# Moving two of eight depthwise convolution chunks from TensorE's banded products to ScalarE products summed on GpSimd

## The chip, the cores and the metric

The kernel runs on one core of a Trainium2 chip. The metric is the time of one launch on the device in microseconds (us). TensorE (PE), VectorE (DVE), ScalarE (ACT), GpSimd (POOL) and SyncE (SP) each work through a list of their own, in order, and wait for each other by semaphores.

## The reference

Two layers of a decoder trunk, 512 tokens of 1024 channels. Layer 0 mixes by a Conformer convolution module, layer 1 by sparse attention, and a gated feed-forward block follows each. The change concerns the convolution module alone:

```python
a, g = jnp.split(h @ w_in + b_in, 2, axis=-1)
u = a * jax.nn.sigmoid(g)
u = depthwise_causal_conv(u, w_dw, taps=31) + b_dw
mu, var = mean(u, -1), mean((u - mu)**2, -1)
u = silu((u - mu) * rsqrt(var + LN_EPS) * ln_g + ln_b)
return u @ w_out
```

All is in float32; a weight matrix product is made of three products of split halves.

## The kernel before

Channels lie on the partitions: 1024 channels are eight chunks of 128 partitions by 512 tokens, in tiles u0 to u7 with 32 columns of zeros ahead.

**Projection.** For each chunk the kernel makes a gate tile and a value tile, each of 24 matmuls (`proj_tile`, lines 282 to 284 or 398 to 400). The weights come by DMA, ScalarE takes their high half (wh, line 222) and VectorE the rest (wl, line 231), one tile ahead. `glu` (line 483) then makes u from the two: gr (line 485), sigmoid on ScalarE (486), ar (488), u (494).

**Convolution, two ways.** Chunks of `DVE_CONV` (0 and 1) are done on VectorE: 31 operations of multiply and add with a weight per partition (lines 501 and 505), the running sum cv in PSUM. They run at a low priority, so that the scheduler puts them into VectorE's gaps. Chunks of `PE_CONV` (2 to 7) are done on TensorE: u is written with the phase of the token first, goes to DRAM and comes back as uf with 16 channels by 8 phases on the partitions (`conv_pe_load`, line 514), and 80 small matmuls with banded weights make the sum (`conv_pe`, line 530, matmul at 544). The bands are loaded on GpSimd's queue into three buffers (line 458). VectorE adds the bias less a shift (548), where nb = bias - shift is made by GpSimd (line 532); ScalarE squares (550); and the result goes back to u through DRAM.

**Layer norm sums.** To keep the variance exact, a shift s, the mean over chunk 0, is taken off (`ln_shift`, line 567). VectorE chunks are shifted (582) and squared (584), and summed over channels by TensorE (lnst, line 593); chunks of TensorE are summed by phase (lng, line 605). `ln_tok` (line 609) copies lnst to rows (612) and transposes it (lnrt, 615); `ln_rows` (line 621) adds the two and makes mean and inverse deviation. Then `ln_out` normalizes chunk by chunk: a chunk of TensorE is read in phase order (line 730), a chunk of VectorE straight (732), then comes the scale (733), Silu twice (739) and the low half (725), and the output projection (lines 373 to 379) begins.

**The order.** The table `CONV_AT` says behind which projection pair (4 to 7, 8 is the end) what is given out: "c4" is the matmuls of chunk 4, "g0" the phase sums of the first TensorE chunk, "n0" and "m0" the shift and square, and the sums, of the first chunk of `LN_ORDER`, "s" the shift, "t" the transpose. From this a scheduler sets each engine's list.

Of the kernel before, what the change touches and what calls it, by code (L numbers as in the profile page):

```python
# [10 lines left out]
F32 = mybir.dt.float32  # L11
# [3 lines left out]
AF = mybir.ActivationFunctionType  # L15
ALU = mybir.AluOpType
# [3 lines left out]
P = 128  # L20
T = 512
# [5 lines left out]
TAPS = 31  # L27
# [8 lines left out]
V_BA, V_BG, V_BDW, V_LNG, V_LNB = 32, 40, 48, 56, 64  # L36
# [15 lines left out]

DVE_CONV = (0, 1)
PE_CONV = (2, 3, 4, 5, 6, 7)
LN_ORDER = (0, 1)
BAND_BUFS = 3
SPLIT = {7: 2}
EH = 2  # L60
CONV_AT = {4: ("s",), 5: ("c2", "c3"), 6: ("g0", "g1", "c4"), 7: ("g2", "n0", "c5"),
           8: ("w", "n1", "m0", "m1", "c6", "g3", "t", "c7", "g4", "g5")}
NLN = len(LN_ORDER)
PH_B = 48
NPH = PH_B + 8 * len(PE_CONV)
WARM0 = 10
# [44 lines left out]
def _two_pi_pieces():  # L111
    rest, out = 2.0 * math.pi, []
    for _ in range(4):
        e = math.floor(math.log2(rest))
        q = 2.0 ** (e - 4)
        piece = math.floor(rest / q) * q
        out.append(piece)
        rest -= piece
    out.append(float(np.float32(rest)))
    return out  # L120
# [3 lines left out]
def trunk(ctx: ExitStack, tc: tile.TileContext, A, out):  # L124
    nc = tc.nc
# [50 lines left out]
    for z in QV_ORDER:  # L176
        if z < 8:
            add("nw_q", z, 1024)
        else:
            w = VW[z - 8]  # L180
# [10 lines left out]
    def after(a, b):  # L191

        if b is not None:
            tc.add_manual_dep(a.ins, b.ins.name, mybir.DependencyInfo(
                mybir.DependencyClass.NoSync, mybir.DependencyReason.DATA), reason="order")
        return a
# [73 lines left out]
    def v(col, n=1):  # L270
        return vec[:, col:col + n]
# [140 lines left out]
    def rope_tables(new, follow):  # L412
        pos = new(I32)
        pf, n, sinT, cosT = (new(F32) for _ in range(4))
        big = 1.5 * 2.0 ** 23
        lim = 3.1415925

        def g(name, *a):
            return lambda: follow(getattr(nc.vector, name)(*a))

        yield lambda: nc.gpsimd.dma_start(pos, A["positions"].partition_broadcast(P))
        yield g("tensor_copy", pf, pos)
        yield g("tensor_scalar", pf, pf, v(V_INVF), None, ALU.mult)
        yield g("tensor_scalar", n, pf, 1.0 / (2.0 * math.pi), big, ALU.mult, ALU.add)
        yield g("tensor_scalar", n, n, -big, None, ALU.add)
        for c in _two_pi_pieces():
            yield g("scalar_tensor_tensor", pf, n, -c, pf, ALU.mult, ALU.add)
        yield g("tensor_scalar", pf, pf, lim, -lim, ALU.min, ALU.max)
        yield lambda: (follow(nc.scalar.activation(sinT, pf, AF.Sin)), follow(nc.scalar.activation(n, pf, AF.Abs)),
                       follow(nc.scalar.activation(cosT, n, AF.Sin, bias=halfpi, scale=-1.0)))  # L430
        yield g("tensor_scalar", sinT, sinT, v(V_SGN), None, ALU.mult)
        yield lambda: (nc.gpsimd.dma_start(angles[0], cosT), nc.gpsimd.dma_start(angles[1], sinT))


    def conv_module():
        acc = new_acc()
        with ExitStack() as cx:
            cp = cx.enter_context(tc.tile_pool(name="cp", bufs=1, side="right"))
            ct = cx.enter_context(tc.tile_pool(name="ct", bufs=2, side="right"))
# [6 lines left out]
            u = [cp.tile([P, 32 + T], F32, tag=f"u{i}", name=f"u{i}") for i in range(NK)]  # L446
            for i in range(NK):
                nc.gpsimd.memset(u[i][:, :32], 0.0)
            vch = [t[:, 32:] for t in u]
            vt = [None] * NK  # L450
# [4 lines left out]
            def load_band(j):  # L455
                t = cp.tile([P, 320, 16], F32, tag="bd", bufs=BAND_BUFS, name=f"bd{j}")
                for h in range(2):
                    tc.keep_in_program_order(nc.gpsimd.dma_start(t[:, 160 * h:160 * h + 160], A["bands"][j, :, 160 * h:160 * h + 160]))
                band[j] = t
# [3 lines left out]
            for k in range(NK):  # L463
# [5 lines left out]
                for m in range(2):  # L469
                    c = slice(k % 2 * 256 + m * P, k % 2 * 256 + (m + 1) * P)  # L470
# [7 lines left out]
            last = {}  # L478
# [4 lines left out]
            def glu(i, pA, pG):  # L483
# [4 lines left out]
                nc.vector.tensor_tensor(ar, pA, R, ALU.mult)  # L488
                if i in PE_CONV:
                    dst = u[i][:, 32:].rearrange("p (r t) -> p t r", r=8)  # L490
# [5 lines left out]
            def wtap(i, j):  # L496
                return wdw[:, i * TAPS + j:i * TAPS + j + 1]

            def conv_dve(i):
                c = pc.tile([P, T], F32, tag="pc", name=f"cv{i}")  # L500
                z = nc.vector.tensor_scalar(c, u[i][:, 2:2 + T], wtap(i, 0), v(V_BDW + i), ALU.mult, ALU.add)
                after(z, last.get("dve"))
                for j in range(1, TAPS):
                    dst = vch[i] if j == TAPS - 1 else c
                    last["dve"] = nc.vector.scalar_tensor_tensor(dst, u[i][:, 2 + j:2 + j + T], wtap(i, j), c,
                                                                 ALU.mult, ALU.add)
                vt[i] = vch[i]

            def views():
# [4 lines left out]
            def conv_pe_load(i):  # L514
                f = cp.tile([P, 8, 68], F32, tag="uf", bufs=len(PE_CONV), name=f"uf{i}")
                nc.gpsimd.memset(f[:, :, :4], 0.0)
                chan, phase = views()
                nc.sync.dma_start(chan, u[i][:, 32:].rearrange("p (r t) -> p r t", r=8))
                last["load"] = nc.sync.dma_start(f[:, :, 4:], phase)
                return f  # L520
# [7 lines left out]
            def conv_pe(j, i, f):  # L528
# [7 lines left out]
                for g0 in range(0, 8, n):  # L536
# [13 lines left out]
                    y = nc.scalar.activation(nb[:, gs], ce[:, gs], AF.Square)  # L550
                    if j == len(PE_CONV) - 2:
                        last["evac"] = {ALU: z, AF: y}
                if j + BAND_BUFS < len(PE_CONV):
                    load_band(j + BAND_BUFS)
                vt[i] = u[i][:, 32:].rearrange("p (r t) -> p r t", r=8)
                backs.append((vt[i], chan))
                if len(ups) == len(PE_CONV):
                    send_backs()
# [29 lines left out]
            def ln_sum(n, q):  # L588
                if n == 0:
                    sh["ps"] = pa.tile([P, T], F32, tag="pst", name="lnst", bufs=1)  # L590
                for e, z in enumerate((vch[LN_ORDER[n]], q)):
                    r0 = 64 * (n % 2) + 32 * e
# [65 lines left out]
            def after_glu(i):  # L658
                if i in PE_CONV:
                    ups[i] = conv_pe_load(i)  # L660
                else:
                    with tc.high_priority(offset=-100000):
                        conv_dve(i)

            def at(i):
                for z in CONV_AT.get(i, ()):
                    if z == "s":
                        ln_shift(LN_ORDER[0])
                    elif z == "t":
# [3 lines left out]
                    elif z[0] == "n":  # L673
                        sh[z] = ln_stat(LN_ORDER[int(z[1:])])
                    elif z[0] == "m":
# [41 lines left out]
            chain = {sh["end"].ins.engine: sh["end"]}  # L717
# [32 lines left out]
            state["behind"] = None  # L750
            pin.clear()
            acc = new_acc()
            follow = dict(chain)

            def table(dt):
                return cp.tile([P, 8, 68], dt, tag="uf", bufs=len(PE_CONV), name=nm("tab")).rearrange(
# [1414 lines left out]
```

## Time and profile before

| | |
|---|---|
| three timed runs | 1196.84, 1197.57, 1198.01 us |
| median | 1197.57 us |
| profiled execution, first to last instruction (span) | 1196.9 us; no other time of it is given |
| median less span | 0.7 us |
| instructions | 21262 |
| granted TensorE clock over the run | 0.999 |

The page gives busy time by engine, then groups of instructions as line, engine, operation, output<-inputs, shape, count, then busy time, the mean of one in ns, and the idle time before them with what ended it. PEld is TensorE's weight load. A row of a timeline is start, length (us), engine, line, operation, and in brackets the idle time ahead and its releaser. A float32 matmul shows as two records. Names in a program's order are tiles with buffer numbers: there u_141 to u_148 are chunks 0 to 7.

### The profile page before, as it was taken

Reading aid. Unit: us, or ns where it says so; the run is one execution under the profiler, and the core shown is the slowest. Engines: PE = TensorE matmul, PEld = TensorE weight load, DVE = VectorE, ACT = ScalarE, POOL = GpSimd, SP = SyncE. Lnnn points to the kernel's source line nnn. Section 1 sums busy time; section 2 is a strip of 40 time slices with the busy share of each in tenths; the row PEclk is TensorE's granted clock in tenths of the full one; section 3 lists DMA queues with packets and bytes.
Section 4 is the critical chain, followed back from the end, with each engine's and each line's share of the span. In section 5 each row is a group of like instructions: output and inputs, shape, how many; then the busy total and the mean of one; then the engine's idle time right before and its main releaser. Section 6 shows DMA issues by size and latency. Waiting matters only on the chain.

```text
span 1196.9 us, 21262 instructions
## 1 busy us (share of the span) xinstructions
PE 1179.3 (99%) x7973; PEld 1003.1 (84%) x7973; DVE 937.0 (78%) x1862; ACT 607.8 (51%) x1146; POOL 234.5 (20%) x355
## 2 busy tenths in 40 slices
PE   9999999999999999999999999999999999999998
PEld 6787778799999888998778867667878999998898
DVE  6996497979999788874567778864597999986876
ACT  5221464455555454553344677873354555554543
POOL 2011002011111101210143466661000111110120
PEclk9999999999999999999999999999999999999999
DMA  8749628257777768753465211017324777775892
GB/s 311 270 116 323 180 89 235 89 154 186 189 185 185 179 185 217 151 156 87 135 164 149 62 28 29 18 27 185 106 88 123 183 191 188 187 195 141 228 189 94
DMA packets 89206, 185.49 MB, mean 155 GB/s; under 512 B 37648, under 2 KB 39312, under 8 KB 87568
## 3 DMA queue, kind: packets, MB, share of 16 engines
q1 hardware_dynamic: 65216, 107.89, 29.3%
q0 software_dynamic: 23888, 76.26, 27.7%
q8 instruction: 62, 1.02, 0.4%
q14 instruction: 40, 0.33, 0.1%
HBM read 168.22 MB, written 5.80 MB: 145 GB/s over the span
## 4 chain that ended last, share of the span: by engine, by line
PE 89%; DVE 6%; issue 2%; ACT 2%; DMA 0%; SPq 0%; DVEq 0%; ACTq 0%
PE st L924 39%; PE pp L282 9%; PE pp L284 9%; PE pp L283 9%; PE O L1893 3%; PE T L1867 3%; PE cpe L544 2%; PE pv L1710 2%; PE S L1836 2%; PE st L283 2%; PE st L282 2%; PE st L284 2%; PE S L1837 1%; DVE wl L231 1%; DVE sol L1108 1%
## 5 line engine op out<-in xcount | busy, mean ns | idle before, releaser
L924 PE MATMUL st<-bo,sh 128*128 128x256 f32 (+1 forms) x952 | 245.6, 333 | 0.4 <-DVE t L960 0.4
L222 ACT ACTIVATE wh<-wr 128x1024 fp32r<-128x1024 f32 (+3 forms) x146 | 151.2, 1035 | 183.0 <-issue 60.6
L231 DVE TENSOR_TENSOR wl<-wr,wh 128x1024 fp32r<-128x1024 f32 (+3 forms) x146 | 174.4, 1194 | 45.4 <-ACT wh L222 44.7
L924 PE MATMUL st<-bo,sl 128*128 128x256 f32 x680 | 191.7, 282 | 0.0
L924 PEld LDWEIGHTS st<-bo,sh 128*128 128x128 f32 x952 | 160.9, 189 | 20.2 <-DVE t L960 1.2
L282 PE MATMUL pp<-hh,wh 128*128 128x512 f32 x400 | 159.3, 401 | 2.6 <-ACT wh L222 2.4
L284 PE MATMUL pp<-hh,wl 128*128 128x512 f32 x400 | 157.1, 396 | 1.4 <-DVE wl L231 1.4
L283 PE MATMUL pp<-hl,wh 128*128 128x512 f32 x400 | 157.4, 395 | 0.0
L924 PEld LDWEIGHTS st<-bo,sl 128*128 128x128 f32 x680 | 129.0, 190 | 0.0
L910 DVE TENSOR_TENSOR sl<-S,sh 128x512 fp32r<-128x512 f32 x136 | 90.6, 688 | 22.3 <-ACT sh L909 22.3
L924 PE MATMUL st<-bo,wh 128*128 128x256 f32 (+1 forms) x408 | 97.4, 316 | 0.0
L282 PEld LDWEIGHTS pp<-hh,wh 128*128 128x128 f32 x400 | 75.2, 188 | 23.7 <-ACT wh L222 4.6
L1854 POOL TENSOR_SCALAR Pm<-Pm,sm,gates 128x512 f32<-128x512 f32 (+3 forms) x128 | 81.3, 648 | 58.2 <-DVE sm L1850 37.8
L284 PEld LDWEIGHTS pp<-hh,wl 128*128 128x128 f32 x400 | 75.1, 188 | 19.9 <-DVE wl L231 2.5
L283 PEld LDWEIGHTS pp<-hl,wh 128*128 128x128 f32 x400 | 75.4, 188 | 17.1 <-issue 0.2
L924 PE MATMUL st<-oz,soh 128*128 128x256 f32 x512 | 88.7, 277 | 0.0
L1840 ACT ACTIVATE Pm<-Pm,mx 128x512 f32<-128x512 f32 (+3 forms) x128 | 70.9, 554 | 31.6 <-DVE mx L1839 30.6
L963 ACT ACTIVATE g<-g 128x512 f32<-128x512 f32 x34 | 21.5, 632 | 112.3 <-DVE g L960 112.3
L924 PEld LDWEIGHTS st<-oz,soh 128*128 128x128 f32 x512 | 77.9, 188 | 0.5
L909 ACT ACTIVATE sh<-S 128x512 fp32r<-128x512 f32 x136 | 77.6, 619 | 0.0
L924 PE MATMUL st<-bo,wl 128*128 128x256 f32 x272 | 75.8, 279 | 0.0
L924 PE MATMUL st<-oz,sol 128*128 128x256 f32 x256 | 71.8, 280 | 0.9 <-DVE sol L1108 0.7
(306 smaller groups left out, 2591.6 us busy)
## 6 DMA issues: line engine op xcount, KB each, us to landing
S<-fw_x POOLq DMA_DIRECT2D x68, 512.0 KB, 5.9
wr<-fw_in SPq DMA_DIRECT2D x46, 512.0 KB
So<-fw_q POOLq DMA_DIRECT2D x38, 512.0 KB, 5.8
bd<-bands POOLq DMA_DIRECT2D x12, 1280.0 KB, 12.2
wr<-fw_q SPq DMA_DIRECT2D x24, 512.0 KB
r<-fw_x SPq DMA_DIRECT2D x34, 256.0 KB
wr<-cw_in SPq DMA_DIRECT2D x14, 512.0 KB
wr<-fw_p SPq DMA_DIRECT2D x12, 512.0 KB
```

What stands on the lines that cost most here:

```text
L222: parted(after(nc.scalar.activation(hi[:, :cols], raws[i][:, :cols], AF.Copy), pin.get(AF)))
L231: parted(after(nc.vector.tensor_tensor(lo[:, :cols], raws[i][:, :cols], hi[:, :cols], ALU.subtract), pin.get(ALU)))
L282: held(nc.tensor.matmul(ps, wh, xh, start=first, stop=False))
L283: held(nc.tensor.matmul(ps, wh, xl, start=False, stop=False))
L284: held(nc.tensor.matmul(ps, wl, xh, start=False, stop=last))
L909: pe(nc.scalar.activation(h_[:, c], z, AF.Copy))
L910: pe(nc.vector.tensor_tensor(l_[:, c], z, h_[:, c], ALU.subtract))
L924: nc.tensor.matmul(out, a[:, k], b, start=f, stop=z, skip_group_check=True))
L1840: kept(nc.scalar.activation(Pt, Pt, AF.Exp, bias=mx, scale=-1.0, accum_out=sm))
L1854: kept(nc.gpsimd.tensor_scalar(Pt, Pt, sm[:, k:k + 1], gates[:, t + k, br * 16 + h:br * 16 + h + 1], ALU.mult, ALU.mult))
L1867: pe(nc.tensor.transpose(pt[:, c:c + P], u["P"][:, o:o + P], ident))
L1893: pe(nc.tensor.matmul(o[par * 64:par * 64 + 64, P * kc:], vf[br][:, kc, g], Us[par][kc], start=False, stop=last))
```

## The change

VectorE now does chunks 0 and 2 and TensorE 4 to 7. Chunks 1 and 3 are done by a new function: for each of 31 taps ScalarE multiplies u, moved by one column per tap, by the weight per partition (the first with the bias, straight into the accumulator pv; the others into a tile tap, of which there are three buffers), and GpSimd adds tap to pv, 30 times; the last add writes to u. pv has one buffer, so both chunks share it. All four are in `LN_ORDER`, so they are shifted, squared and summed straight; the table `CONV_AT` is written anew. Two more edits keep the transfers of the rotary tables on GpSimd's queue behind the last of the adds. Lines below the new function are 13 higher than before.

```diff
-DVE_CONV = (0, 1)
-PE_CONV = (2, 3, 4, 5, 6, 7)
-LN_ORDER = (0, 1)
+DVE_CONV = (0, 2)
+POOL_CONV = (1, 3)
+PE_CONV = (4, 5, 6, 7)
+LN_ORDER = (0, 1, 2, 3)
...
-           8: ("w", "n1", "m0", "m1", "c6", "g3", "t", "c7", "g4", "g5")}
+           8: ("w", "m0", "m1", "c6", "n2", "n3", "m2", "m3", "t", "g2", "c7", "g3")}
...
-        yield lambda: nc.gpsimd.dma_start(pos, A["positions"].partition_broadcast(P))
+        yield lambda: follow(nc.gpsimd.dma_start(pos, A["positions"].partition_broadcast(P)))
...
+            def conv_pool(i):
+                c = cp.tile([P, T], F32, tag="pacc", name=f"pv{i}")
+                for j in range(TAPS):
+                    z = c if j == 0 else ct.tile([P, T], F32, tag="tap", bufs=3, name=f"tap{i}")
+                    src, w = u[i][:, 2 + j:2 + j + T], wtap(i, j)
+                    if j == 0:
+                        nc.scalar.activation(z, src, AF.Identity, scale=w, bias=v(V_BDW + i))
+                    else:
+                        nc.scalar.activation(z, src, AF.Copy, scale=w)
+                        last["pool"] = nc.gpsimd.tensor_tensor(vch[i] if j == TAPS - 1 else c, c, z, ALU.add)
+                vt[i] = vch[i]
...
-                        conv_dve(i)
+                        (conv_pool if i in POOL_CONV else conv_dve)(i)
...
-            follow = dict(chain)
+            follow = dict(chain) | {last["pool"].ins.engine: last["pool"]}
```

More of the change, by code (lines that the diff above doesn't have):

```diff
@@ L60 @@
 EH = 2
-CONV_AT = {4: ("s",), 5: ("c2", "c3"), 6: ("g0", "g1", "c4"), 7: ("g2", "n0", "c5"),
-           8: ("w", "n1", "m0", "m1", "c6", "g3", "t", "c7", "g4", "g5")}
+CONV_AT = {4: ("s",), 5: ("c4",), 6: ("c5", "g0"), 7: ("n0", "n1", "g1"),
+           8: ("w", "m0", "m1", "c6", "n2", "n3", "m2", "m3", "t", "g2", "c7", "g3")}
 NLN = len(LN_ORDER)
```

## The prediction

> **What bounds the kernel now.** I read the page first, then the chain of work that ended last from 100 to 145 us, the stretches of 20 us, the timelines of VectorE, ScalarE and GpSimd in the convolution stage, and the groups of instructions by form. About 0.2% of the time, 2.4 us, is what a measurement of this kernel can tell from no change.
>
> ```profile
> span 1196.9 us, 21262 instructions
> PE 1179.3 (99%) x7973; PEld 1003.1 (84%) x7973; DVE 937.0 (78%) x1862; ACT 607.8 (51%) x1146; POOL 234.5 (20%) x355
> ```
>
> TensorE has no free time over the whole run, so a shift of one stage goes through to the end. All that the change touches lies between 35 and 165 us. The chain there, as start, length and what:
>
> ```profile
> 100.39 1.00 PE lng L605 x8
> ...
> 117.69 0.24 PE pp L284
> 117.93 0.98 PE lng L605 x4
> 118.91 4.82 PE cpe L544 x160
> 123.73 0.99 PE lnst L593 x8
> 124.72 4.82 PE cpe L544 x160
> 129.54 0.98 PE lng L605 x4
> 130.52 0.59 PE lnrt L615 x4
> ```
>
> One chunk on TensorE costs 4.82 us of the chain (80 matmuls, two records each). The last projection ends at 117.93. After it come two chunks and the sums, and at 130.52 the transpose of the statistics (lnrt), which I use as the milestone: it and the last chunk's matmuls stand behind it in both orders. The other engines, by stretch:
>
> ```profile
> 40.00:60.00 20.00, 18.62 (x79) 14.50 (x78) 18.80 (x25) 4.46 (x5) 0.00 (x0) 1.00 0.57 193
> 60.00:80.00 20.00, 20.00 (x109) 15.42 (x109) 18.55 (x25) 5.00 (x7) 0.00 (x0) 1.00 0.51 152
> 80.00:100.00 20.00, 19.87 (x345) 17.61 (x341) 19.54 (x27) 3.76 (x5) 6.14 (x8) 1.00 0.63 218
> 100.00:120.00 20.00, 19.89 (x260) 15.09 (x260) 9.53 (x14) 3.77 (x5) 3.63 (x5) 1.00 0.89 287
> ...
> 140.00:160.00 20.00, 19.41 (x89) 14.43 (x87) 18.60 (x27) 14.74 (x19) 0.00 (x0) 1.00 0.39 112
> 160.00:180.00 20.00, 19.93 (x86) 15.88 (x85) 18.94 (x30) 11.78 (x18) 0.00 (x0) 1.00 0.32 104
> ```
>
> The columns after the length are the busy times of PE, weight load, VectorE, ScalarE and GpSimd, then the granted clock. VectorE is full until 100 us with its own two chunks; ScalarE and GpSimd are nearly empty there. The clock stays at 1.00.
>
> **What the change takes from TensorE.** Before the last projection ends there stood three chunks (2, 3, 4) and 1.00 us of phase sums; now there stand two (4, 5) and one chunk's sums, 0.98 us by the row at 117.93. So the projections could end at 117.93 - 4.82 = 113.1. Behind them before: 0.98 + 4.82 + 0.99 + 4.82 + 0.98 = 12.6 us. Now: 0.98 (phase sums), 0.99 (chunks 0 and 1), 4.82 (one chunk), 0.98 (chunk 2), 0.98 (phase sums), 0.98 (chunk 3; a lone chunk costs as much as two together) = 9.7 us. By TensorE alone lnrt stands at 122.8, 7.7 us earlier.
>
> The layer norm behind it gains too, because two chunks lose their strided read:
>
> ```profile
> L730 DVE TENSOR_TENSOR c<-u,lnb 128x512 f32<-128x512 f32 x6 | 7.1, 1179 | 0.0
> L732 DVE TENSOR_TENSOR u<-u,lnb 128x512 f32<-128x512 f32 x2 | 1.4, 682 | 0.0
> ```
>
> 2 x (1.18 - 0.68) = 1.0 us, on a path where VectorE is last. Two phase sums fewer behind the last chunk I put at 0.5 us (one pair of 512 columns, half of 0.98). So up to 9.2 us are offered.
>
> **The wait that comes with it.** TensorE takes its instructions in order. Here the place behind the last projection, before (uf and nb belong to chunks on TensorE, u_141 and u_142 are chunks 0 and 1):
>
> ```order
> L605 MATMUL lng<-uf_723,ph 32x512
> L605 MATMUL lng<-nb_1016,ph 32x512
> L544 MATMUL cpe_1178<-uf_976,bd_846 64x64 x80
> L593 MATMUL lnst<-u_141,onesb 32x512
> L593 MATMUL lnst<-lsq_1173,onesb 32x512
> L593 MATMUL lnst<-u_142,onesb 32x512
> L593 MATMUL lnst<-lsq_1281,onesb 32x512
> L544 MATMUL cpe_1291<-uf_1140,bd_936 64x64 x80
> L605 MATMUL lng<-uf_976,ph 32x512
> L605 MATMUL lng<-nb_1176,ph 32x512
> L615 MATMUL lnrt<-cc,rows 128x128 x4
> ```
>
> And now, from the sums of chunks 0 and 1 on (u_143 is chunk 2 of VectorE, u_144 is chunk 3 of GpSimd):
>
> ```order
> L606 MATMUL lnst<-u_141,onesb 32x512
> L606 MATMUL lnst<-lsq_1250,onesb 32x512
> L606 MATMUL lnst<-u_142,onesb 32x512
> L606 MATMUL lnst<-lsq_1253,onesb 32x512
> L557 MATMUL cpe_1283<-uf_1219,bd_299 64x64 x80
> L606 MATMUL lnst<-u_143,onesb 32x512
> L606 MATMUL lnst<-lsq_1371,onesb 32x512
> L618 MATMUL lng<-uf_1219,ph 32x512
> L618 MATMUL lng<-nb_1281,ph 32x512
> L606 MATMUL lnst<-u_144,onesb 32x512
> L606 MATMUL lnst<-lsq_1374,onesb 32x512
> L628 MATMUL lnrt<-cc,rows 128x128 x4
> ```
>
> The sum of chunk 3 now stands ahead of lnrt, and so ahead of the 80 matmuls of chunk 7: all of them wait until GpSimd has added 30 products twice. ScalarE has a wait of the same kind. Its order at the end of the projections, before:
>
> ```order
> L222 ACTIVATE wh_1106<-wr_943 128x1024
> L486 ACTIVATE gr_1134<-gr_1134,vec 128x512
> L584 ACTIVATE lsq_1173<-u_141 128x512
> L550 ACTIVATE nb_1016<-uf_723 128x512
> L486 ACTIVATE gr_1262<-gr_1262,vec 128x512
> L584 ACTIVATE lsq_1281<-u_142 128x512
> L550 ACTIVATE nb_1176<-uf_976 128x512
> L612 ACTIVATE rows<-lnst 128x512
> ```
>
> Now, from the last gate (gr) on, with the taps of chunk 3:
>
> ```order
> L487 ACTIVATE gr_1257<-gr_1257,vec 128x512
> L518 ACTIVATE tap_795<-u_144,wdw 128x512
> L518 ACTIVATE tap_798<-u_144,wdw 128x512
> L597 ACTIVATE lsq_1371<-u_143 128x512
> L518 ACTIVATE tap_801<-u_144,wdw 128x512
> L518 ACTIVATE tap_804<-u_144,wdw 128x512
> L518 ACTIVATE tap_807<-u_144,wdw 128x512
> L518 ACTIVATE tap_810<-u_144,wdw 128x512
> L563 ACTIVATE nb_1281<-uf_1219 128x512
> L518 ACTIVATE tap_813<-u_144,wdw 128x512
> L223 ACTIVATE wh_1499<-wr_1268 128x1024
> L518 ACTIVATE tap_816<-u_144,wdw 128x512
> ```
>
> The last eight products stand behind the gate of the last projection, so eight adds can't start before it, however fast GpSimd is.
>
> **The prices.** When the parts are there, from the timelines:
>
> ```profile
> 34.94 0.75 DVE L494 SCALAR_TENSOR_TENSOR u<-ar,vec,gr 128x512 f32<-128x512 f32 x1
> 118.76 0.72 ACT L486 ACTIVATE gr<-gr,vec 128x512 f32<-128x512 f32 x1 [10.36 <-DVE gr L485]
> 120.50 0.69 DVE L582 TENSOR_TENSOR u<-u,s 128x512 f32<-128x512 f32 x1
> 121.29 0.63 ACT L584 ACTIVATE lsq<-u 128x512 f32<-128x512 f32 x1 [1.81 <-DVE u L582]
> 125.09 0.58 ACT L612 ACTIVATE rows<-lnst 128x512 f32<-128x512 f32 x1
> ```
>
> Chunk 1's input is whole at 35.7. From the end of the adds to lnrt it is subtraction and square (120.50 to 121.92, 1.4 us), the sum on TensorE (0.98) and the copy to rows (124.72 to 125.67, 1.0): 3.4 us. A tap on ScalarE is a copy with a scale by partition, like the split of x; an add on GpSimd has two inputs:
>
> ```profile
> L316 ACT ACTIVATE hh<-x,vec 128x512 fp32r<-128x512 f32 x16 | 11.1, 714 | 3.7 <-DMA x<-xT 2.2 <-DVE x L762 1.5
> L532 POOL TENSOR_TENSOR nb<-ph,sp 128x512 f32<-128x512 f32 x6 | 6.1, 1042 | 63.0 <-DMA sp<-swap 63.0
> L1598 POOL TENSOR_TENSOR sc<-sc,cc 128x512 f32<-128x512 f32 x3 | 3.8, 1282 | 0.0
> L1613 POOL TENSOR_TENSOR sc<-sc,cl 128x512 f32<-128x512 f32 x3 | 3.1, 1049 | 0.5 <-DVE sm L1850 0.5
> ```
>
> 62 taps are 62 x 0.714 = 44 us of ScalarE, in about 100 us of which it uses some 17: it isn't the bound. Between which prices an add lies is the question of this case. The two cheap groups (1.04 and 1.05) read one value of an operand over a whole inner row (L532 stretches ph over 64 columns, L1613 stretches cl over 32). L1598 reads both operands element by element, as an add of a tap does, and works in place as the adds do. I take 1.28 and keep 1.04 as the other end. The page GPSIMD Engine Reference of the Trainium skill (section Performance versus the Vector engine) measures 4497 ns for an add of 2048 columns; a quarter of it, 1.12 us, is an estimate by that page, between the rows, and by it the sum below would end near 1195 us.
>
> Each add reads what the one before wrote and waits for its semaphore. What such a link costs GpSimd no row shows; a chain on VectorE shows it there:
>
> ```profile
> 84.84 4.05 POOL L532 TENSOR_TENSOR nb<-ph,sp 128x512 f32<-128x512 f32 x4 [62.99 <-DMA sp<-swap]
> 86.53 5.49 DVE L505 SCALAR_TENSOR_TENSOR cv<-u,wdw,cv 128x512 f32<-128x512 f32 x7
> 88.83 2.14 POOL L458 DMA_DIRECT2D bd<-bands  x4
> ```
>
> Seven taps in 5.49 us, the last 0.75 long, are 0.79 each: 0.04 more than one lasts. I take 0.06 for GpSimd (0 to 0.15), so 1.34 an add. The rows show also that a VectorE tap, one input of which lies in PSUM, costs GpSimd nothing: four adds beside them took 4.05, 1.01 each.
>
> It is otherwise beside VectorE work with two inputs in SBUF, the low halves of the weights (L231) above all:
>
> ```profile
> 684.77 2.46 POOL L1854 TENSOR_SCALAR Pm<-Pm,sm,gates 128x512 f32<-128x512 f32 x4 [2.27 <-PE T L1867]
> 724.99 0.67 DVE L1592 TENSOR_TENSOR sc<-sc,cm 128x512 f32<-128x512 f32 x1
> 725.24 3.10 POOL L1854 TENSOR_SCALAR Pm<-Pm,sm,gates 128x512 f32<-128x512 f32 x4 [1.38 <-DVE sm L1850]
> 725.69 1.16 DVE L1569 TENSOR_TENSOR St<-q,St 64x512 fp32r<-64x512 f32 x1
> 793.39 3.43 POOL L1854 TENSOR_SCALAR Pm<-Pm,sm,gates 128x512 f32<-128x512 f32 x4 [1.14 <-DVE sm L1850]
> 795.36 1.23 DVE L231 TENSOR_TENSOR wl<-wr,wh 128x1024 fp32r<-128x1024 f32 x1 [1.26 <-ACT wh L222]
> L231 DVE TENSOR_TENSOR wl<-wr,wh 128x1024 fp32r<-128x1024 f32 x11 | 13.4, 1218 | 0.0
> ```
>
> The same group of four on GpSimd takes 2.46 us alone, 3.43 beside one L231 (0.97 more) and 3.10 beside two shorter ones (0.32 each), while one of those grew from 0.67 to 1.16. The page SBUF — State Buffer of the Trainium skill (section Who interferes with whom) states the rule: a VectorE instruction with two SBUF inputs and a GpSimd one that reads SBUF can't both hold the shared ports, the second "fully blocks". The trace agrees; by the rule the eleven would cost GpSimd 11 x 1.22 = 13.4 us (estimate), where by the measured 0.97 they cost 10.7.
>
> In the stage there are these eleven L231 and about ten shorter ones (six u, four subtractions): 10.7 + 10 x 0.32 = 13.9 us at most. The gap of 0.06 and the start of each add let some of them pass, so I take 10 (5 to 14).
>
> **The sum.** First add at 35.7 + 2 x 0.71 = 37.1. Sixty adds at 1.34: 80.4. In the same queue four nb (4.05) and one band load (two issues, half of 2.14, 1.1): 5.1. Idle: chunk 3 has to wait for the one accumulator, which ScalarE refills only after the last add of chunk 1 (two taps, about 1.5 us), and nb for sp, near 85: 3 together. Contention 10. The adds end at 37.1 + 80.4 + 5.1 + 3 + 10 = 135.6, lnrt stands at 139.0, 8.5 us later than 130.52. Less 1.0 and 0.5 of the tail: +7.0. Queued behind the wait on TensorE is the whole rest; no later slack takes it back at 99% busy. The span was 1196.9, the median of the runs shown 1197.57, 0.7 more, which I carry over: **1204.6 us**.
>
> Costed at nothing: four band loads and two round trips through DRAM fewer (no wait of the chain on them is seen); the positions and angle transfers, now behind the last add on GpSimd's queue (their tables are used in the attention hundreds of us later); the feed-forward's weight loads in that queue, since GpSimd is idle from 140 to 180. ScalarE's wait for a tap buffer (three) holds the wh split behind it by at most one add, 1.3 us, of the 5.8 that a projection tile gives (24 matmuls of 0.24, the row at 117.69); if that cover is gone, TensorE waits that much per tile, up to ten times.
>
> **The rivals.**
>
> *The add is cheap (1.04 to 1.12).* For it: nine of the twelve two-input operations of GpSimd in the groups above. Against: none of the nine reads both operands element by element. The skill's quarter of 4497 ns falls to this side. Then sixty adds at 1.10 are 66 us and GpSimd would be through at 37.1 + 66 + 5.1 + 3 + 10 = 121.2, but the last eight wait for the gate: 118.76 - 4.82 + 0.72 + 0.71 = 115.4, plus 8 x 1.10 = 124.2, with 1 us of contention 125.2. lnrt at 128.6, 1.9 earlier, with the tail 3.4: 1194.2. This is the faster side; it decides when the adds end before 130.52 - 3.4 + 1.5 = 128.6, which is an add of 1.22 with its link. Chance 0.22.
>
> *VectorE waits instead of GpSimd.* At 725.69 it lost 0.49 of the 0.64 that both lost. Then GpSimd loses nothing, but of the 21 operations 17 stand ahead of the last projection, and 17 x 0.49 = 8.3 us fall on VectorE, which has about 4.7 us to spare (20 - 9.53 in the stretch to 120, less the 4.82 by which it shrinks and about 1); so the projections end 3.6 us later, at 116.7, the gate and the next tap at 119.0, the eight adds at 119.0 + 10.7 = 129.7, lnrt at 133.1: +2.6 - 1.5 = +1.1, 1198.7. No change that can be told. An add midway, 1.16, gives about the same by the first sum (128.4, 131.8, -0.2: 1197.4). Chance 0.16 for both.
>
> *Dense adds as forecast.* Chance 0.62. Contention of 5 to 14 instead of 10 is -5 to +4 us, a link of 0.02 to 0.12 instead of 0.06 is -2.4 to +3.6; taken as independent, -5.5 to +5.4: its own range is 1199.1 to 1210.0.
>
> **How the numbers follow.** 1204.6 is the likeliest case. The range runs from the cheap case's 1194.2 to the top of the dense one's own, 1210. Faster by over 0.2%: 0.22, the first rival; within: 0.16, the second; slower: 0.62.
>
> **What would show it.** In the changed profile: the adds' group at 1.28 on GpSimd, start to start near 1.35 and longer beside L232; TensorE idle in front of the last lnst and of lnrt, released by VectorE and ScalarE, whose own wait is for GpSimd; lnrt near 139; the stages after 165 us of the same length. Wrong: adds at 1.05 to 1.15, or lnrt below 130; or TensorE losing its time earlier, waiting for wl in the projections.

## The result, and the profile after

The changed kernel takes **1213.53 us** (median of 4 runs, 1213.16 to 1214.02), the kernel before in the same comparison 1197.79 (4 runs, 1196.84 to 1199.08); beside the runs further down it had medians of 1197.34 to 1198.52. The ratio is 1.013 with a 95% interval of 1.0116 to 1.0145. Slower was forecast, and from the wait that is there; but it is 15.7 us and not 7.0, above the top of the range, 1210.0. The profiled execution has a span of 1212.2 us, 15.3 more than the one of before. One execution of the changed kernel, in the last comparison, took 4051.62 us and is left out.

The page first: TensorE's busy time is the same, though it has two chunks' matmuls less to do (the run with two taps, further down, has the same number of them and is busy for 1170.1 us; here some of them run at a lowered clock); its share is not.

```profile
span 1212.2 us, 20770 instructions
...
PE 1178.2 (97%) x7653; PEld 996.4 (82%) x7653; DVE 947.9 (78%) x1862; ACT 648.9 (54%) x1208; POOL 320.7 (26%) x407
```

Then the stretches of 20 us, in the columns of before (PE, weight load, VectorE, ScalarE, GpSimd, granted clock, DMA share, GB/s):

```profile
80.00:100.00 20.00, 18.38 (x272) 15.57 (x272) 19.02 (x24) 10.88 (x16) 17.68 (x15) 1.00 0.51 147
100.00:120.00 20.00, 20.00 (x265) 15.18 (x262) 19.25 (x22) 11.86 (x18) 18.98 (x14) 1.00 0.34 109
120.00:140.00 20.00, 6.99 (x81) 2.95 (x78) 6.42 (x5) 10.36 (x16) 18.57 (x14) 0.71 0.53 145
140.00:160.00 20.00, 17.67 (x219) 12.99 (x218) 7.10 (x20) 7.77 (x13) 0.00 (x0) 0.77 0.31 81
```

Between 120 and 140 us only GpSimd is full. TensorE is busy for 6.99 us, and the granted clock averages 0.71 and then 0.77. In the profile of before the same stretch, with the same columns, is:

```profile
120.00:140.00 20.00, 18.13 (x493) 15.59 (x490) 6.31 (x15) 5.84 (x10) 0.00 (x0) 1.00 0.74 195
```

TensorE's timeline shows what it waits for:

```profile
115.37 0.62 PE L618 MATMUL lng<-uf,ph 128*32 128x512 f32 x1
...
117.21 4.89 PE L557 MATMUL cpe<-uf,bd 128*64 128x64 f32 x160
127.63 1.06 PE L606 MATMUL lnst<-u,onesb 128*32 128x512 f32 x1 [5.53 <-DVE u L595]
...
132.73 1.04 PE L618 MATMUL lng<-nb,ph 128*32 128x512 f32 x2 [1.48 <-ACT nb L563]
139.77 1.06 PE L606 MATMUL lnst<-u,onesb 128*32 128x512 f32 x1 [5.99 <-DVE u L595]
...
143.09 1.11 PE L628 MATMUL lnrt<-cc,rows 128*128 128x128 f32 x4 [0.69 <-ACT rows L625]
144.14 7.10 PE L557 MATMUL cpe<-uf,bd 128*64 128x64 f32 x160
...
158.14 0.50 PE L374 MATMUL pp<-a,wh 128*128 128x512 f32 x1 [0.55 <-ACT a L752]
```

The projections end at 115.4 (forecast 113.1). Then TensorE waits 5.53 us for chunk 2 and 5.99 for chunk 3, each time for the subtraction on VectorE (L595); lnrt stands at 143.09 (forecast 139.0). Behind it the 80 matmuls of chunk 7 take 7.10 us where before they ran from 131.04 to 136.79, 5.75. The out-projection starts at 158.14, 14.3 us later than the 143.85 of before. GpSimd's timeline shows why chunk 3 is last:

```profile
37.63 47.08 POOL L519 TENSOR_TENSOR pv<-pv,tap 128x512 f32<-128x512 f32 x29 [15.42 <-ACT tap L518]
...
87.99 1.92 POOL L519 TENSOR_TENSOR pv<-pv,tap 128x512 f32<-128x512 f32 x1 [1.93 <-ACT pv L516]
89.87 4.06 POOL L545 TENSOR_TENSOR nb<-ph,sp 128x512 f32<-128x512 f32 x4
...
96.23 41.42 POOL L519 TENSOR_TENSOR pv<-pv,tap 128x512 f32<-128x512 f32 x27
137.73 1.26 POOL L519 TENSOR_TENSOR u<-pv,tap 128x512 f32<-128x512 f32 x1
```

The adds run from 37.63 to 138.99 with hardly a gap. Chunk 2 is VectorE's own, its last tap (the first line below) is done at 118.37, and still it comes late:

```profile
117.62 0.75 DVE L506 SCALAR_TENSOR_TENSOR u<-u,wdw,cv 128x512 f32<-128x512 f32 x1
123.09 0.70 ACT L487 ACTIVATE gr<-gr,vec 128x512 f32<-128x512 f32 x1
123.83 2.20 DVE L495 SCALAR_TENSOR_TENSOR u<-ar,vec,gr 128x512 f32<-128x512 f32 x1 [4.26 <-ACT gr L487]
125.87 1.71 DVE L595 TENSOR_TENSOR u<-u,s 128x512 f32<-128x512 f32 x1
```

Its subtraction (L595) stands in VectorE's list behind the u of the last gate. That gate has its input at 119.57 but runs on ScalarE only at 123.09, behind three taps that each wait for GpSimd to free a buffer. So the wait for chunk 2, too, comes from the pace of the adds.

The groups by form, from 28 to 145 us (count, then busy time and mean ns):

```profile
L519 POOL TENSOR_TENSOR pv<-pv,tap 128x512 f32<-128x512 f32 x58 | 87.5, 1508 | 21.6 <-ACT tap L518 15.4 <-ACT pv L516 1.9
L232 DVE TENSOR_TENSOR wl<-wr,wh 128x1024 fp32r<-128x1024 f32 x12 | 21.0, 1752 | 8.2 <-ACT wh L223 8.1
L495 DVE SCALAR_TENSOR_TENSOR u<-ar,vec,gr 128x512 f32<-128x512 f32 x8 | 10.9, 1368 | 5.4 <-ACT gr L487 5.4
L595 DVE TENSOR_TENSOR u<-u,s 128x512 f32<-128x512 f32 x4 | 5.8, 1476 | 2.5 <-POOL u L519 2.5
```

The chain of waits has the add alone; beside VectorE it is longer:

```profile
59.82 1.29 POOL pv L519
...
61.18 2.17 POOL pv L519
...
65.13 1.29 POOL pv L519
...
66.50 2.15 POOL pv L519
```

The first of the two low halves beside them, on VectorE's timeline:

```profile
60.10 2.09 DVE L232 TENSOR_TENSOR wl<-wr,wh 128x1024 fp32r<-128x1024 f32 x1 [0.54 <-ACT wh L223]
```

Alone an add takes 1.29 us, as forecast; beside the low halves (L232, at 60.10 and 65.73) 2.15 and more. VectorE's operations with two inputs in SBUF lose as well: the low halves 1752 ns instead of 1218, u 1368 instead of 1050, the subtractions 1476 instead of 693. The last two of these before, over the same time:

```profile
L494 DVE SCALAR_TENSOR_TENSOR u<-ar,vec,gr 128x512 f32<-128x512 f32 x8 | 8.4, 1050 | 1.6 <-ACT gr L486 1.6
L582 DVE TENSOR_TENSOR u<-u,s 128x512 f32<-128x512 f32 x2 | 1.4, 693 | 0.0
```

One wait more appears far behind the change, from 640 to 700 us in the attention: TensorE's product S (L1849) waits for VectorE's maximum mx. Before has no such row:

```profile
PE S L1849 <- DVE mx L1852: 1.5, 2, 0.8
```

### The profile page after: what moved, and what is told of

The parts are those of the page before. It is cut to its first block, busy times and chain, and to the rows that moved or that the text cites. A ratio compares the mean times of both kernels' runs of the same rounds, so it can differ in the third digit from the quotient of the medians.

```text
span 1212.2 us, 20770 instructions
## 1 busy us (share of the span) xinstructions
PE 1178.2 (97%) x7653; PEld 996.4 (82%) x7653; DVE 947.9 (78%) x1862; ACT 648.9 (54%) x1208; POOL 320.7 (26%) x407
## 4 chain that ended last, share of the span: by engine, by line
PE 80%; DVE 8%; POOL 4%; ACT 3%; issue 2%; DMA 1%; SPq 0%; POOLq 0%; DVEq 0%; ACTq 0%
PE st L937 39%; PE pp L283 7%; PE pp L285 7%; PE pp L284 7%; POOL pv L519 4%; PE O L1906 3%; PE T L1880 3%; PE S L1849 2%; PE st L284 2%; PE st L283 2%; PE st L285 2%; PE S L1850 1%; DVE wl L232 1%; DVE cv L506 1%; ACT wh L223 1%
## 5 line engine op out<-in xcount | busy, mean ns | idle before, releaser
L232 DVE TENSOR_TENSOR wl<-wr,wh 128x1024 fp32r<-128x1024 f32 (+3 forms) x146 | 180.8, 1238 | 53.1 <-ACT wh L223 52.9
L519 POOL TENSOR_TENSOR pv<-pv,tap 128x512 f32<-128x512 f32 x58 | 87.5, 1508 | 21.6 <-ACT tap L518 15.4
L898 POOL DMA_DIRECT2D S<-fw_x x34 | 20.0, 590 | 265.7 <-DVE sl L923 264.2
```

Of the source, the lines that this page charges most:

```text
L232: parted(after(nc.vector.tensor_tensor(lo[:, :cols], raws[i][:, :cols], hi[:, :cols], ALU.subtract), pin.get(ALU)))
L519: last["pool"] = nc.gpsimd.tensor_tensor(vch[i] if j == TAPS - 1 else c, c, z, ALU.add)
```

## The experiments

**Half the change.** Chunk 3 goes back to TensorE. Here and in the other runs with one chunk the tile rows has one buffer instead of three, to make room.

```diff
-POOL_CONV = (1, 3)
-PE_CONV = (4, 5, 6, 7)
-LN_ORDER = (0, 1, 2, 3)
+POOL_CONV = (1,)
+PE_CONV = (3, 4, 5, 6, 7)
+LN_ORDER = (0, 1, 2)
...
-CONV_AT = {4: ("s",), 5: ("c4",), 6: ("c5", "g0"), 7: ("n0", "n1", "g1"),
-           8: ("w", "m0", "m1", "c6", "n2", "n3", "m2", "m3", "t", "g2", "c7", "g3")}
+CONV_AT = {4: ("s",), 5: ("c3",), 6: ("c4", "g0"), 7: ("n0", "n1", "g1", "c5"),
+           8: ("w", "m0", "m1", "c6", "g2", "n2", "m2", "t", "c7", "g3", "g4")}
...
```

> Only chunk 1 goes to GpSimd; chunk 3 goes back to TensorE (five chunks there, two on VectorE). Theory A (the loss is the wait for the second GpSimd chunk, which ends too late because GpSimd and VectorE slow each other; TensorE's idle time then costs clock as well): the 30 adds end near 88 us, long before anyone needs them, TensorE has no idle gap and no lowered clock between 100 and 160 us, one chunk's 4.82 us and about 0.5 us of strided read are gained, and the time is 1191 to 1194 us, below the kernel before. Rival B (what hurts is VectorE's own loss beside GpSimd, which makes the low halves of the weights late for the projections): the gain is eaten up in the projections, 1196 to 1199 us.

Measured: 1197.63 us, ratio 0.9997 (0.9988 to 1.0006). The time is Rival B's, its mechanism isn't: the projections end at 113.6, and the clock stays at 1.00 from 40 to 160 us. TensorE's timeline:

```profile
129.30 0.65 PE L628 MATMUL lnrt<-cc,rows 128*128 128x128 f32 x4 [2.16 <-ACT rows L625]
...
141.84 0.50 PE L374 MATMUL pp<-a,wh 128*128 128x512 f32 x1 [0.55 <-ACT a L752]
```

The out-projection starts 2.0 us earlier than before. The rest of the gain went into a wait of 2.16 us for rows, which ScalarE had queued behind the split of the out-projection's weights, and that waits for its transfer until 127.71; into chunk 2's sum, which stands alone (0.98); and into 1.8 us of waiting for mx in the attention.

**The order on TensorE.** Chunk 7 ahead of chunk 3's sum.

```diff
-           8: ("w", "m0", "m1", "c6", "n2", "n3", "m2", "m3", "t", "g2", "c7", "g3")}
+           8: ("w", "m0", "m1", "c6", "n2", "m2", "g2", "c7", "n3", "m3", "t", "g3")}
```

> As the changed kernel, but chunk 7's matmuls stand ahead of the sum of chunk 3 and of the transpose of the statistics. Theory A (TensorE idles because its order puts 80 ready matmuls behind the wait for GpSimd): the adds still end near 139 us and the transpose still comes near 143, but the 7.1 us of chunk 7 and its sums no longer stand behind it, so the out-projection starts some 6 to 7.5 us earlier than 158.1 and the time is 1206 to 1208 us. Rival B (VectorE and ScalarE are as late as TensorE, so chunk 7's eviction and squares become the last wait): less than 3 us come back, 1211 us or more.

Measured: 1208.45 us, ratio 1.0091 (1.0074 to 1.0108): 5.1 us back, between the two, and the start by Theory A's 6.8.

```profile
127.58 1.06 PE L606 MATMUL lnst<-u,onesb 128*32 128x512 f32 x1 [5.56 <-DVE u L595]
...
132.19 1.73 PE L557 MATMUL cpe<-uf,bd 128*64 128x64 f32 x26 [1.98 <-DMA uf<-swap]
...
143.28 0.66 PE L628 MATMUL lnrt<-cc,rows 128*128 128x128 f32 x4 [0.51 <-ACT rows L625]
...
151.36 0.50 PE L374 MATMUL pp<-a,wh 128*128 128x512 f32 x1 [0.55 <-ACT a L752]
```

lnrt stays at 143.3 and chunk 7 is hidden in front of it. But it can't start before 132.2, because its own input comes late: the last gate stands on ScalarE behind taps that wait for GpSimd (it runs at 123.04 here, at 123.09 in the changed kernel), and then comes the round trip through DRAM (uf). The order alone doesn't save the change.

**The clock.** Matmuls of zeros in the idle time; g2 is moved between them.

```diff
+                    elif z[0] == "x":
+                        warm(sh["w"], int(z[1:]), last["conv"])
...
-           8: ("w", "m0", "m1", "c6", "n2", "n3", "m2", "m3", "t", "g2", "c7", "g3")}
+           8: ("w", "m0", "m1", "c6", "n2", "n3", "x22", "m2", "x12", "g2", "x24", "m3", "t", "c7", "g3")}
```

> As the changed kernel, with 58 matmuls of zeros (a product that nobody reads) in TensorE's idle time behind chunk 6 and around the sums of chunks 2 and 3. Nothing else moves. Theory A (the idle time lowers the granted clock, and that costs time by itself): the clock stays at 1.00 from 120 to 160 us, chunk 7 takes about 4.8 us instead of 7.1 and the sums about 0.1 us less each, so the time is 1210 to 1211.5 us. Rival B (the low clock only shows in idle time, or the matmuls of zeros delay as much as they save): 1213 to 1214 us.

Measured: 1211.5 us, ratio 1.0116 (1.0098 to 1.0133); 2.0 us less by the medians, though the intervals overlap. The profile shows it more sharply:

```profile
143.55 0.66 PE L628 MATMUL lnrt<-cc,rows 128*128 128x128 f32 x4 [0.69 <-ACT rows L625]
144.13 4.89 PE L557 MATMUL cpe<-uf,bd 128*64 128x64 f32 x160
...
155.91 0.50 PE L374 MATMUL pp<-a,wh 128*128 128x512 f32 x1 [0.55 <-ACT a L754]
```

With the clock at 1.00 in both stretches, chunk 7 takes 4.89 us instead of 7.10, and from lnrt to the out-projection it is 12.36 us instead of 15.05. Theory A holds: idle time on TensorE cost 2.7 us behind its end. In the profile after the granted clock is 0.50 from 125.2 to 132.0 us and from 135.4 to 149.1, so chunk 7, from 144.14 on, has half the clock for its first 5.0 us; half of that is 2.5 us (an estimate), and it lost 2.2. The Trainium skill, page TensorE: Matmul & The Clock Gate (Part 1, on the warmup), says that the clock is halved after an idle window of some 3.4 us; the gaps of 5.53 and 5.99 us agree, though less idle time was enough elsewhere (last section).

**Contention.** The low halves of the projections' weights beside the adds are left out; the one tile of zeros in their place is made once, as raw less raw.

```diff
-        lo = wp.tile([P, 1024], F32R, tag="wl", name=f"wl{i}", bufs=2)
+        lo = state["zero"] if 4 < i < 18 else wp.tile([P, 1024], F32R, tag="wl", name=f"wl{i}", bufs=2)
...
+        if 4 <= i < 18:
+            if "zero" not in state:
+                state["zero"] = lo
+            else:
+                lo = state["zero"]
+                los.add(i)
         split[i] = (hi, lo)
...
+        src = raws[i] if lo is state.get("zero") else hi
...
```

> As the changed kernel, but the low halves of the first projections' weights are left out from the fifth weight tile on (one tile of zeros stands for them), so that VectorE has no subtraction of 128 x 1024 with two inputs in SBUF beside the adds; TensorE's matmuls are all still there. Theory A (GpSimd loses about 0.8 us beside each of these 12, VectorE's u and subtractions cost it the rest): the adds' mean falls from 1.51 to 1.36 to 1.42 us, the adds end 7 to 10 us earlier, near 130, and the time is 1203 to 1207 us. Rival B (GpSimd is late by its own price and the link from add to add, and the low halves hardly matter to it): the mean stays above 1.46, the adds end after 136, and the time is 1211 us or more.

Measured: 1202.18 us, ratio 1.0039 (1.0026 to 1.0052). The group of adds in this run:

```profile
L526 POOL TENSOR_TENSOR pv<-pv,tap 128x512 f32<-128x512 f32 x58 | 79.0, 1361 | 19.6 <-ACT tap L525 14.6 <-ACT pv L523 0.9
```

The adds end at 128.9, 10.1 us earlier: 8.5 from these adds (58 x 0.147) and 1.6 because the first starts at 36.0; the last add takes 0.9 longer here, beside a low half of the out-projection, and as much idle time is saved. Theory A, a little past its good end. The control is the kernel before with the same edit:

> The kernel before, with the same low halves of the weights left out as in the run on contention (from the fifth weight tile on, one tile of zeros for all). The control for that run, whose time fell by 11.3 us against the changed kernel's 1213.5. Theory A (what that run gained is contention between GpSimd and VectorE): without work on GpSimd the low halves are nearly free, because TensorE waits some 1.4 us for them in the stretch from 40 to 60 us only, so the time is 1195 to 1197.5 us. Rival B (the subtractions by themselves hold up the projections, with or without GpSimd): 1192 us or less.

Measured: 1196.29 us, ratio 0.9992 (0.9983 to 1.0001). The time is Theory A's, but a part of Rival B is in it: the out-projection starts at 139.98 there, 3.9 us earlier than in the kernel before, and 1.5 us of that is lost again to mx in the attention. So of the 11.3 us that the run above gained at the same place (158.14 to 146.82), some 7.4 (11.3 less 3.9) are contention; the sixty adds by themselves, busy for 82.4 us instead of 90.0, give 7.6.

**What TensorE offers.** First without the adds:

```diff
-                        last["pool"] = nc.gpsimd.tensor_tensor(vch[i] if j == TAPS - 1 else c, c, z, ALU.add)
+                        if j == TAPS - 1:
+                            last["pool"] = nc.gpsimd.tensor_tensor(vch[i], c, z, ALU.add)
```

> As the changed kernel, but of the 30 adds of each of its two chunks only the last is done (the products of 29 taps are computed on ScalarE and left out of the sum), so GpSimd is idle in the convolution stage. It shows what the change offers when GpSimd is neither late nor in VectorE's way. Theory A (forecast's first step is right, and what is lost is lost through GpSimd's work): the low halves' subtraction is back at about 1.22 us, the projections end near 113 us, TensorE doesn't wait, the out-projection starts near 134.6 (143.85 less 9.2) and the time is 1187.5 to 1190.5 us. Rival B (the taps on ScalarE by themselves hold up gates and weights): the projections end at 114.5 or later and the time is 1192 us or more.

Measured: 1195.25 us, ratio 0.9983 (0.9974 to 0.9992), with the projections ending at 117.6: Rival B. The low halves are back at 1220 ns, but nothing paces the taps any more:

```profile
44.00:52.00 8.00, 5.37 (x23) 3.76 (x21) 7.34 (x11) 8.00 (x13) 0.00 (x0) 0.99 0.19 76
52.00:60.00 8.00, 8.00 (x28) 6.45 (x29) 7.79 (x11) 8.00 (x14) 0.94 (x1) 0.79 0.41 133
```

ScalarE (the fourth busy time) is full, the weights' splits stand behind its taps, TensorE idles 2.6 us and the clock drops. TensorE waits 2.13 us more at 98 us, for the input of chunk 5 (uf). So this run didn't measure the offer. The second leaves out the products as well:

```diff
-                for j in range(TAPS):
+                for j in (0, TAPS - 1):
                     z = c if j == 0 else ct.tile([P, T], F32, tag="tap", bufs=3, name=f"tap{i}")
```

> As the changed kernel, but chunks 1 and 3 have only their first and last tap (29 products on ScalarE and 29 adds on GpSimd are left out for each), so neither engine has more to do than before. It measures the first step of the forecast: what TensorE alone offers. Forecast: projections end near 113.1, the transpose of the statistics stands at 122.8, the out-projection starts near 134.6 and the time is 1188 to 1190 us. Theory A (the offer is nearly whole, and the run without adds lost it to ScalarE, whose unhindered taps stood ahead of the weights' splits): 1188 to 1191 us. Rival B (part of the offer was never there, because chunks 4 and 5 now stand one projection nearer to their own gate and wait for the round trip of their input through DRAM, as chunk 5 did for 2.1 us without the adds): TensorE waits for uf, the out-projection starts after 136 and the time is 1191.5 to 1194 us.

Measured: 1190.14 us, ratio 0.9941 (0.9925 to 0.9956).

```profile
112.85 0.62 PE L618 MATMUL lng<-uf,ph 128*32 128x512 f32 x1
...
122.06 0.66 PE L628 MATMUL lnrt<-cc,rows 128*128 128x128 f32 x4
122.65 5.19 PE L557 MATMUL cpe<-uf,bd 128*64 128x64 f32 x160
...
134.74 0.50 PE L374 MATMUL pp<-a,wh 128*128 128x512 f32 x1 [0.55 <-ACT a L752]
```

Forecast were 113.1, 122.8 and 134.6. Theory A: the offer is there, whole, and the round trips don't touch it. Of the 9.1 us at the out-projection's start 7.5 are left in the time (1197.61 for the kernel before beside it); TensorE waits 1.5 us for mx in the attention. What the change lost, it lost to the work that stands in for TensorE's.

**Taps shared with VectorE.** The order of the second run, and chunk 3's last 8 taps on VectorE.

```diff
+SHARE = {3: 23}
-                for j in range(TAPS):
+                e = SHARE.get(i, TAPS)
+                for j in range(e):
...
+                if e < TAPS:
+                    d = pc.tile([P, T], F32, tag="pc", name=f"cv{i}")
+                    after(nc.vector.tensor_scalar(d, u[i][:, 2 + e:2 + e + T], wtap(i, e), None, ALU.mult), last.get("dve"))
+                    for j in range(e + 1, TAPS):
+                        last["dve"] = nc.vector.scalar_tensor_tensor(d, u[i][:, 2 + j:2 + j + T], wtap(i, j), d,
+                                                                     ALU.mult, ALU.add)
+                    last["dve"] = nc.vector.tensor_tensor(vch[i], d, c, ALU.add)
```

> The changed kernel's split into four, two and two chunks, with two edits: chunk 7's matmuls ahead of the sum of chunk 3, and the last 8 of chunk 3's 31 taps on VectorE (its own partial sum, added at the end), so that GpSimd does 22 adds for it. Theory A (the wait for the second chunk is the bound, and work taken off its end moves the end): GpSimd ends near 127 us instead of 139, VectorE joins the parts near 128, the transpose comes near 131.5, the out-projection starts near 139 to 140.5 and the time is 1192.5 to 1196 us. Rival B (VectorE, which has chunk 2 until 118 us and loses to GpSimd, becomes as late as GpSimd was): the transpose comes after 134 and the time is 1198 us or more.

Measured: 1206.64 us, ratio 1.0077 (1.0063 to 1.009), in Rival B's place. Theory A's own times came about 1 us late (GpSimd ends at 128.2, the parts are joined by 129.3), but lnrt came only at 145.1:

```profile
128.77 1.06 PE L615 MATMUL lnst<-u,onesb 128*32 128x512 f32 x1 [6.99 <-DVE u L604]
...
133.70 1.72 PE L566 MATMUL cpe<-uf,bd 128*64 128x64 f32 x26 [2.30 <-DMA uf<-swap]
...
145.14 0.66 PE L637 MATMUL lnrt<-cc,rows 128*128 128x128 f32 x4
```

In the second run's order chunk 3's sum stands behind chunk 7, and chunk 7 waits for its input, whose gate VectorE finishes only at 127.2, behind its new taps. Another wait, then, is as late as GpSimd was: the last gate and its round trip.

**One chunk, better placed.** The first half-change again, with the sum of chunk 2 next to those of 0 and 1:

```diff
-CONV_AT = {4: ("s",), 5: ("c3",), 6: ("c4", "g0"), 7: ("n0", "n1", "g1", "c5"),
-           8: ("w", "m0", "m1", "c6", "g2", "n2", "m2", "t", "c7", "g3", "g4")}
+CONV_AT = {4: ("s",), 5: ("c3",), 6: ("c4", "g0"), 7: ("g1", "n0", "n1", "c5"),
+           8: ("w", "n2", "m0", "m1", "m2", "c6", "t", "g2", "c7", "g3", "g4")}
```

> Again only chunk 1 on GpSimd, but the sum of chunk 2 stands with those of chunks 0 and 1 behind chunk 5's matmuls, so that ScalarE's copy of the sums (rows) comes ahead of the split of the out-projection's weights, which waits for its transfer. Theory A (the run before lost 2.16 us because rows stood behind that split, and the rest of its gain to where the lowered clock falls in the attention): the transpose of the statistics no longer waits for ScalarE, the out-projection starts 1.5 to 2.2 us earlier than the 141.84 us of that run, at 139.6 to 140.4, and the time is 1194 to 1196.5 us. Rival B (another wait takes its place, or the tail's chain through VectorE sets the start): the start stays at 141 us or later and the time at 1197 to 1198.5.

Measured: **1194.94 us**, ratio 0.9978 (0.9968 to 0.9988): the only kernel of the study with the whole convolution that is faster than the one before. But not as Theory A had it. lnrt comes at 127.88 without a wait for rows, and still the out-projection starts at 142.18, in Rival B's place: this execution lost 2.3 us of TensorE's time between 44 and 52 us and the clock behind it (0.79). What it has ahead of the first half-change lies behind that start, 1051.2 us to the end instead of 1054.8: there is no wait for mx in it (1.8 us there), and the granted clock from 640 to 700 us was 1.00 in this execution and 0.97 in the other.

The same with another chunk:

```diff
-DVE_CONV = (0, 2)
-POOL_CONV = (1,)
+DVE_CONV = (0, 1)
+POOL_CONV = (2,)
```

> One chunk on GpSimd as in the run with the early sum, but it is chunk 2 instead of chunk 1, so that taps and adds begin some 10 us later, and VectorE has chunks 0 and 1 as before the change. Theory A (that run lost 2.4 us of TensorE's time between 44 and 56 us, and a lowered clock of 3.4 us behind it, because the taps begin just where ScalarE and VectorE have to make two weight tiles in a row): TensorE's idle time there is back at about 1.4 us with the clock at 1.00, the adds end before 100 us and the time is 1191.5 to 1194 us. Rival B (the same loss appears wherever the taps begin): 1194 to 1197 us.

Measured: 1196.91 us, ratio 0.9993 (0.9984 to 1.0002): Rival B.

```profile
44.00:52.00 8.00, 6.08 (x23) 4.30 (x22) 7.41 (x10) 6.17 (x9) 5.06 (x4) 0.90 0.16 53
52.00:60.00 8.00, 8.00 (x33) 6.43 (x32) 6.97 (x9) 5.20 (x8) 7.61 (x6) 0.89 0.35 121
```

TensorE idles 1.9 us and the clock drops, although ScalarE's work for the chunk began only at 45 us. The out-projection starts at 141.03, and 1.5 us go to mx.

**The wait in the attention.** VectorE's order there is not written by hand, and the scheduler moved some ten instructions of it when the convolution changed. One matmul of zeros more moves them back:

```diff
-WARMS = {"t": 2, "r": 5}
+WARMS = {"t": 3, "r": 5}
```

> The changed kernel with three instead of two matmuls of zeros behind the spread of the mean (about 0.2 us of TensorE, read by nobody). The source of the attention is the same, but with this the scheduler puts VectorE's instructions there in the order that the kernel before has (in the changed kernel some ten of them, on cl and gates, stand further back). Theory A (the last 1.5 us of the changed kernel's loss, which appear only near 660 us, are TensorE waiting in S for VectorE's maximum mx, and come from that order): no such wait between 640 and 700 us, and 1 to 2 us less than the changed kernel in the run beside this, 1211.5 to 1212.5 us. Rival B (they come from where the lowered clock falls, which changes from run to run): the wait or its 1.5 us stay, and the time is within 0.5 us of the run beside this.

> The changed kernel itself, for comparison on the same chip: 1213 to 1214 us by both theories, with 1.5 us of TensorE's time between 640 and 700 us spent waiting for mx.

Measured: 1212.03 us (ratio 1.0111, 1.0094 to 1.0128) against 1213.16 (three executions; 1.0117, 1.01 to 1.0133) for the changed kernel again. The medians are 1.1 us apart, the intervals overlap, so the time alone doesn't decide it. The traces do: TensorE's waits from 640 to 700 us in the run with the third matmul are

```profile
PE bc L1332 <- DVE qraw L1334: 1.9, 1, 1.9
PE psc L1588 <- ACT t L1885: 0.9, 1, 0.9
PE T L1880 <- DVE pcl L1642: 0.2, 1, 0.2
```

without mx, which again has 1.5 us in the changed kernel beside it. The granted clock from 640 to 700 us is 1.00 in both executions, so Rival B's cause is absent, and from the out-projection's start to the end they take 1051.2 and 1053.3 us. Over the study the profiles with VectorE's order of before (before, the changed kernel without low halves, early sum, third matmul) have no such wait; with the other order it is 1.4 to 1.8 us, but for the run on the clock (0.3).

## Why the prediction missed

By its own steps, against the profile after (GpSimd's adds are busy 87.5 us, and 2.5 for the last add of each chunk: 90.0):

| step | forecast | measured |
|---|---|---|
| first add starts | 37.1 | 37.63 |
| sixty adds alone | 60 x 1.28 = 76.8 | 60 x 1.285 = 77.1 |
| links, nb, band load, idle | 3.6 + 5.1 + 3 = 11.7 | 138.99 - 37.63 - 90.0 = 11.4 |
| lost by GpSimd beside VectorE | 10 (5 to 14) | 90.0 - 77.1 = 12.9 |
| adds end | 135.6 | 138.99 |
| from there to lnrt | 3.4 | 4.1 |
| lnrt to the end of the run | 1.5 less than before | 15.3 - 12.6 = 2.7 more |

The miss in the profiled execution is 15.3 - 7.0 = 8.3 us: 3.4 in the adds' end, 0.7 from there to lnrt, 4.2 behind it.

- *What TensorE offers*: right. The run with two taps has all three places within 0.8 us.
- *The wait, its place and who is queued behind it*: right. lnst of chunk 3 waits for GpSimd, and lnrt and chunk 7 behind it. The dense add at 1.28 was right too, which settles the first rival: start to start was 1.36 (59.82, 61.18) to 1.37 (65.13, 66.50), a link of 0.07 to 0.08 where I took 0.06.
- *Contention 10 us, all of it on GpSimd*: inside its bounds (5 to 14) but mis-sized by 2.9 us, and the split was wrong. Both engines lose. Of the twelve low halves in the table by form, ten stand beside adds and are left out in the run without them: they cost GpSimd 8.5 / 10 = 0.85 us each, and average 1.84 us on VectorE, 0.63 more than before; together 1.48. The Trainium skill, page SBUF — State Buffer (Who interferes with whom), says that one holds the shared ports and the other waits; the trace agrees, and shows that each waits in turn. The low half that starts at 60.10 meets an add that ends at 61.11, and is done at 62.19 instead of 61.32; the next add starts at 61.18 and is done at 63.35 instead of 62.47. So the second rival's mechanism was there as well, on top of the first sum and not in its place. Since GpSimd was never short of work at the end, what VectorE lost (projections at 115.4 against 112.9 without the taps) lies beside GpSimd's wait and added nothing to the end.
- *"The clock stays at 1.00"*: this is the step that failed by itself. It was read from the profile of before, where TensorE hardly idles, and carried over into a forecast whose point was that TensorE would idle. I priced the wait and not what the wait does to the work behind it: 15.05 - 12.36 = 2.7 us behind lnrt by the run with the matmuls of zeros, and part of the 0.7 ahead of it, where sums took 1.06 us a record instead of 0.62.
- *"The stages after 165 us of the same length"*: failed by 1.5 us, the wait for mx. I compared the order of the instructions around the change only; VectorE's order in the attention had moved as well.
- *ScalarE's wait for a tap buffer, at most one add and only for the weights' split*: too small, and it missed the gate. The last gate ran 3.5 us after its input was there, behind three taps, and chunk 2's sum stood at 127.63 us, where the run with two taps has it at 119.50. In the time GpSimd's later end hid this.
- *Two round trips fewer, at nothing*: right for the time, but the last one has no room once the adds hold up the gates: both runs that let TensorE go on to chunk 7 found its input not yet there.

3.4 + 0.7 + 2.7 + 1.5 = 8.3. The clock and the attention, which were not in the sum at all, make about half of it. Had their costs been among the bounds, the range would have held. One reading was loose, without effect: the 17 us of ScalarE are those of 40 to 120 us, 80 us and not 100.

## What to carry to other kernels

Work moved to an idle engine is paid for by the whole chain that it makes there: sixty dependent adds need 101 us of GpSimd, so the second chunk was late whatever TensorE did, and what could be had (0.2%) came from moving half as much. When a forecast contains idle time of TensorE, price the clock behind it, and ask which transfer or gate is late next before a new order is trusted. When a scheduler sets the order, compare it over the whole program, not only around the edit.

## What was not expected of the hardware

- A VectorE instruction and a GpSimd one with all inputs in SBUF slow each other: 2.15 us for an add that takes 1.29 alone, 1.75 on average for a low half that takes 1.22.
- Short idle times lower the clock too, and not in every execution. With 1.4 to 1.5 us of idle TensorE between 44 and 52 us (before, the first half-change, two taps) the clock there and in the 8 us behind stayed at 1.00; with 1.9 (chunk 2 on GpSimd) it was 0.90 and 0.89; with 1.7 (the run on the clock), 2.3 (early sum) and 2.6 (no adds) 0.79 behind it, with 2.45 (the changed kernel again) 0.63; in the profile after, with 2.2, it stayed at 1.00.
- What sorts these executions better is the idle time within 3.4 us. In the profile after the granted clock is either 1.00 or 0.50 and changes at 125.2, 132.0, 135.4 and 149.1 us: 6.8, 3.4 and 13.7 us apart, all multiples of 3.4. In the stretch of 3.4 us that ends where the clock fell, TensorE was busy for 0.80 us (no adds, 48.5 to 51.9), 1.53 (the changed kernel again, 47.7 to 51.1) and 1.67 (chunk 2, 46.9 to 50.3); with 1.92 (profile after, 50.1 to 53.5) and 2.02 (before, 48.5 to 51.9) it stayed at 1.00. In the profile after the 2.2 us fell into two such stretches. The limit isn't sharp: with 1.84 the clock stayed in one execution (the first half-change, 125.3 to 128.7) and fell in another (the run on the order, 142.3 to 145.7), and with 1.46 it stayed once (the third matmul, 80.2 to 83.6).
